# A hybrid encoder layer on one core: queries and keys stored as fp16 parts, and the order of its first stages

## The chip, the cores and the metric

The kernel runs on one core of a Trainium2 chip. The metric is the device time of one execution in microseconds (us). Three runs of the kernel before took 2835.52 to 2839.13 us, median 2836.63. A separate execution was recorded by the hardware profiler; all lines of the profile come from it. The engines are PE (TensorE: matmuls; PEld is its weight load), DVE (VectorE), ACT (ScalarE), POOL (GpSimd) and SP (SyncE, which issues most DMAs). Each engine works through its own instructions in order.

## The reference

One layer on x of 2048 tokens by 1024, with 256 memory tokens:

```python
y = rmsnorm(x, g_mix) @ w_in                     # q, k, v (512 each), a, g (512 each)
q, k = partial_rotary(q), partial_rotary(k)      # 8 heads of 64, the first 16 of each head turned
att = dilated_sliding_attention(q, k, v)         # windows (128,1), (512,4), (2048,16), softmax-weighted
u = a * sigmoid(g); conv = silu(layernorm(depthwise_conv31(u) + conv_b))
h = x + concat(att, conv) @ w_out
h = h + cross_attention(rmsnorm(h, g_x), rmsnorm(mem, g_mem)) @ w_xo     # 4 heads of 256
h = h + relu(rmsnorm(h, g_mlp) @ w_up)**2 @ w_down                       # 4096 hidden
out = rmsnorm(h, g_final)
```

The pattern (window, dilation) splits the tokens into `dilation` strided sequences; in each, a query sees keys at a distance of at most window / (2 x dilation) = 64.

## The kernel before

**Numbers.** Values that enter a matmul are split into two parts, high and low, and a product is three matmuls: high by high, high by low, low by high (`mm3`, L390 to L394). For the linear layers the parts are fp16, each tile scaled by a power of two. The scale is found on the chip: `pow2` (L194) takes a sum or maximum over a tile, its inverse root, and keeps the exponent. `wscale` (L325) does this for each 1024 x 128 tile of w_in by itself, with a DVE pass, a small matmul `p`, a POOL power and DVE steps. `wsplit2` (L377) writes the high part on ACT (L379) and the low part on DVE (L380); `wsplit_views` (L345) does it with a permutation of columns for the rotary tiles (L347 to L350). The queries and keys are the exception: they are kept as fp32r (fp32 bits, read by TensorE as fp32r) high and low parts, each key tile holding high rows in partitions 0 to 63 and low rows in 64 to 127, so a score takes two matmuls (L1112 and L1113 for the dilation 16, L1258 for the others), of 256 or 128 columns each.

**Stages, by the time of the profiled execution.**
- 0 to about 131 us: projections of the memory (`memory`, L554), in fp32r, with `xprep` (L528) of the first two quarters of x: load 512 tokens, norm, transpose, split into fp16 parts, and write the transposed x back (xscr).
- to about 230: the gated units `glu` 0 and 1 (L722; a unit g and a unit a, each 1024 x 128 weights times 512 tokens, for two quarters of x), with `xprep` of the other two quarters.
- to about 440: `lin_qk` (L845), eight units: kr and qr hold the first 16 dimensions of every head (rotary), k0, q0, k1, q1, k2, q2 the other 48. Each loads its weight tile, scales and splits it, multiplies it with four quarters of x, turns the rotary ones (L906 to L910), and splits the result (keys L927 and L928, queries L919 and L920). It stores the parts to DRAM: kscr (keys, ordered by token modulo 16), qscr (queries), qfar (queries ordered by token modulo 16). ACT issues the stores of the high parts, SP those of the low parts. The far tiles are stored in two halves. The rope tables are loaded for kr and again for qr.
- Beside these units run, woven in by rates: `scan` (L220), which loads all of w_up and w_out in 40 tiles of 512 KB and squares them on ACT (sjunk, L227) to bound the scales; `vscale` (L761), column norms of the v weights (two halves squared on ACT, added on POOL, summed by matmuls vss, L778); and the first quarter of the convolution (DVE, L409).
- to about 548: glu 2, v for the first two pairs of heads' halves (`lin_v`, L789), glu 3, the first half of the second v unit, whose weights are written to vscr and read back (wvr) for the second half.
- to about 780: the attention of the first 512 queries together with the dilation 16 for all queries (`att`, `att_far`, L1093), woven with the rest of v and of the gated units.
- from about 780: four `post` stages (L1488), each output projection, cross-attention and MLP for 512 tokens, woven with the attention and convolution of the next 512. In the first of them `scan_down` (L242) loads w_down in 32 tiles (scand) and squares them on ACT (L249).

**What sets the order.** The program is written as generators that `pipeline`, `weave` and `run` interleave by hand-set rates; `pinned` and `after` tie an instruction behind the last one of an engine. A scheduler then orders the instructions of each engine, with the tiles of the pools as constraints: a tile with 3 buffers can be loaded again only when its third-last use is over. SP issues its DMAs in that fixed order, so a load that waits for a buffer holds up all loads behind it; ACT, too, holds up a weight split behind a square that waits for its load.

All DMAs are issued by one helper, so most show as L58.

Of the kernel before, what the change touches and what calls it, by code (L numbers as in the profile page):

```python
# [10 lines left out]
F32 = mybir.dt.float32  # L11
# [37 lines left out]
def hybrid_layer(ctx, tc, A, out):  # L49
# [58 lines left out]
    kscr = dr.tile([2, HD, H, 16, 160], F32R, name="kscr")  # L108
    qscr = dr.tile([2, HD, H, S], F32R, name="qscr")
    qfar = dr.tile([2, HD, H, 16, P], F32R, name="qfar")  # L110
# [39 lines left out]
    cst.tile([P, 96], F32, name="cpad")  # L150
# [82 lines left out]
    def loads_ahead(gens):  # L233

        next(gens[0])
        for i, g in enumerate(gens):
            if i + 1 < len(gens):
                next(gens[i + 1])
            yield
            next(g, None)  # L240
# [238 lines left out]
    xna[2] = pool("x2", stack=mems, side="right")  # L479
    mwp = pool("memw", stack=mems, side="right")  # L480
# [15 lines left out]
    def load_nat(sp, src, name, bufs=10):  # L496

        t = [sp.tile([P, 512], F32, tag="nat", name=f"{name}_{e}", bufs=bufs) for e in range(2)]
        for e in range(2):
            dma(t[e], src[:, 512 * e:512 * e + 512])  # L500
        return t
# [26 lines left out]
    def xprep(sp, n):  # L528
        xtiles(n)
        nat = [load_nat(sp, A["x"][0, 512 * n + P * j:512 * n + P * (j + 1), :], f"xn{n}_{j}") for j in range(4)]  # L530
        r = rstd_nat(sp, nat, f"x{n}")
        rb = ps("c", f"rb{n}")
        bcast_rows(rb, r, 4)
        rbs = sp.tile([P, 512], F32, tag="rbs", name=f"rbs{n}", bufs=1)
        ACT.copy(rbs, rb)
        yield
        for k in range(KC):
            pt = ps("a", f"xt{n}_{k}")
            for j in range(4):
                PE.transpose(pt[:, j * P:(j + 1) * P], nat_cols(nat[j], k), ident)  # L540
            xt = sp.tile([P, 512], F32, tag="xt", name=f"xts{n}_{k}", bufs=3)
            DVE.tensor_copy(xt, pt)
            dma(xscr[k][:, 512 * n:512 * (n + 1)], xt)
            xv = sp.tile([P, 512], F32, tag="xv", name=f"xv{n}_{k}", bufs=2)
            DVE.scalar_tensor_tensor(xv, pt, gmix[:, k:k + 1], rbs, op0=ALU.mult, op1=ALU.mult)
            ACT.copy(XH_[k, n], xv)
            POOL.tensor_tensor(XL_[k, n], xv, XH_[k, n], op=ALU.subtract)
            yield

# [4 lines left out]
    def memory(sp):  # L554
# [24 lines left out]
        def wtiles(name, shape=(P, 8, P)):  # L579
            i = cnt[0] % 4  # L580
            cnt[0] += 1
            if i < 2:
                return [pl.tile(list(shape), dt, tag=t, name=f"m{t}_{name}", bufs=b)
                        for pl, t, dt, b in ((wp, "raw", F32, 3), (mwp, "whi", F32R, 2), (mwp, "wlo", F32R, 2))]
            return [xpool(q, j, 2, f"m{q}{j}_{name}", shape, dt)
                    for q, j, dt in (("h", i - 2, F32), ("h", i, F32R), ("l", i, F32R))]
# [174 lines left out]
    def vscale():  # L761

        for pr in range(4):
# [6 lines left out]
            POOL.tensor_tensor(sq[0], sq[0], sq[1], op=ALU.add)  # L770
            POOL.tensor_tensor(sq[0][:, 0:2], sq[0][:, 0:2], sq[0][:, 2:4], op=ALU.add)
            yield
            yield
            with ExitStack() as st:
                after(st, "pe", "dve")
                pc = ps("c", f"vss{pr}")
                for q in range(2):
                    PE.matmul(pc[:, 0:1], sq[0][:, q], ones[:, 0:1], start=q == 0, stop=q == 1)  # L778
# [65 lines left out]

    def lin_qk(isq, c):  # L845

        base = 0 if isq else DATT
        nm = f"{'q' if isq else 'k'}{c}"
        key = ("q" if isq else "k", c)
        v = w_in.rearrange("(k p) m -> p k m", p=P)  # L850
        raw = wp.tile([P, 8, P], F32, tag="raw", name=f"raw_{nm}", bufs=3)
        if c == "r":
            for k in range(KC):
                dma(raw[:, k, :].rearrange("p (h j) -> p h j", j=16),
                    v[:, k, base:base + DATT].rearrange("p (h d) -> p h d", d=HD)[:, :, 0:16])
            yield
            yield from wscale(raw, key)
            yield
            views = [(lambda t, x=x: t.rearrange("p k (h x j) -> p k h x j", x=2, j=8)[:, :, :, x, :],
                      lambda t, x=x: t[:, :, x * 64:(x + 1) * 64].rearrange("p k (j h) -> p k h j", h=H))  # L860
                     for x in range(2)]
            hi, lo = two(wsplit_views(raw, wcol(key, 0), nm, views))
        else:
            for p, h, d, m in segs(c):
                dma(raw[:, :, p:p + m], v[:, :, base + h * HD + d:base + h * HD + d + m])
            yield
            yield from wscale(raw, key)
            yield
            hi, lo = two(wsplit2(wp, raw, nm, wcol(key, 0)))

        def rope(n):
            t = []
            for i in range(2 if c == "r" else 0):
                t.append(t2(f"rope{i}_{nm}{n}"))
                dma(t[i], A["rope"][i, :, 512 * n:512 * (n + 1)])
            return t

        nxt = rope(0)
        yield

        def store(d, t, tail, q=None):

            if c != "r":
                for p, h, d0, m in segs(c):
                    dma(f(d[(slice(d0, d0 + m), h) + tail]), f(t[p:p + m]), q)
            else:
                v = d[(slice(0, 16), slice(0, H)) + tail]
                dma(f(v.rearrange("d h s -> (d h) s" if len(tail) == 1 else "d h r i -> (d h) r i")), f(t), q)

        w = 64 if isq else 80  # L890
        for n in range(NG):
            hf = n // 2
            i0 = 0 if isq or hf else PADI
            if n % 2 == 0:
                far = [lbk.tile([P, 16, 80], F32R, tag=f"st{x}", name=f"st{x}_{nm}{hf}", bufs=2)[:, :, 0:w] for x in "hl"]
                if not isq:
                    for t in far:
                        POOL.memset(f(t[:, :, 64:] if hf else t[:, :, 0:PADI]), 0.0)
            rc = nxt
            if n + 1 < NG:  # L900
                nxt = rope(n + 1)
            pt = linear(hi, lo, n)
            if c == "r":
                ct, sn = rc
                sw = t2(f"sw_{nm}{n}")
                ACT.copy(sw[0:64], pt[64:128])  # L906
                ACT.copy(sw[64:128], pt[0:64])
                last["dve"] = DVE.tensor_tensor(ct, pt, ct, op=ALU.mult)
                POOL.tensor_tensor(sn, sw, sn, op=ALU.mult)
                POOL.tensor_tensor(ct, ct, sn, op=ALU.add)  # L910
# [3 lines left out]
            sl = slice(i0 + 32 * (n % 2), i0 + 32 * (n % 2) + 32)  # L914
            fh, fl = (t[:, :, sl].rearrange("p r i -> p i r") for t in far)
            if isq:
                o = t2(f"qh_{nm}{n}", F32R)
                l = lbk.tile([P, 512], F32R, tag="ql", name=f"ql_{nm}{n}", bufs=3)
                ACT.activation(o, src, AF.Copy, scale=wcol(key, 2))  # L919
                last["dve"] = DVE.scalar_tensor_tensor(l, src, wcol(key, 2), f(o), op0=ALU.mult, op1=ALU.subtract)  # L920
                cols = (slice(512 * n, 512 * (n + 1)),)
                for z, (t, ft) in enumerate(((o, fh), (l, fl))):
                    store(qscr[z], t, cols, None if z else nc.scalar)
                    POOL.tensor_copy(f(ft), f(t).rearrange("p (i r) -> p i r", r=16))
# [945 lines left out]
```

## Time and profile before

| | us |
|---|---|
| median of 3 runs | 2836.63 |
| lowest, highest | 2835.52, 2839.13 |
| profiled execution | 2834.45 |
| its span, first to last instruction | 2832.7 |
| PE busy | 2692.5 |
| DVE busy | 2063.9 |
| ACT busy | 1311.4 |
| POOL busy | 451.7 |

The mean granted clock of TensorE over the span is 0.974; 462.09 MB are moved. The page gives busy time by engine, the span in 40 slices of 70.8 us, the DMA queues (q1 is SP's, q10 ACT's), and the chain of work that ended last. The windows view gives the busy time of each engine in a stretch that is asked for, with the granted clock and the share of the 16 DMA engines that was busy (it can come out a little over 1). The line view groups instructions by line, engine and operation: busy time, mean ns of one, and idle time ahead of them with what ended it. The view of waits sums such idle time by pair. A matmul's duration includes its way through the array; consecutive ones overlap, so PE's busy time is less than their sum.

### The profile page before, as it was taken

The page shows a single profiled execution, that of the slowest core. Times are in us where ns is not written, and L with a number is a line of the kernel's source. Part 1 is how long each engine was busy: PE and PEld are TensorE (multiplying, and loading weights), DVE is VectorE, ACT ScalarE, POOL GpSimd, SP SyncE. Part 2 cuts the span into 40 slices and gives each one's busy share as a digit, 9 for nine tenths or more (in the row PEclk, how much of TensorE's full clock was granted, in tenths as well). Part 3 has the DMA queues.
Part 4 walks back from the last instruction along what each step waited for, and adds up shares of the span by engine and source line. Part 5 has one row for each costly group of instructions (what it writes and reads, how often), then busy time and mean ns, then how long its engine had stood idle before and what let it go on. Part 6 is the DMA issues. An engine that isn't in the chain of part 4 may idle for free.

```text
span 2832.7 us, 41746 instructions
## 1 busy us (share of the span) xinstructions
PE 2692.5 (95%) x15482; PEld 1486.3 (52%) x15482; DVE 2063.9 (73%) x3757; ACT 1311.4 (46%) x2169; POOL 451.7 (16%) x499
## 2 busy tenths in 40 slices
PE   8877899899878999999999999999999999999998
PEld 7743346677644554544555555455455544444443
DVE  6765675655557998766898876579988656579997
ACT  5646321165557543453554345345443444455443
POOL 1024431121210211130011203100201130000000
PEclk9988899999998999999999999999999999999999
DMA  9899996559887544455444455454445355233341
GB/s 274 264 264 277 252 219 173 173 167 239 208 274 226 142 132 128 138 148 149 148 130 129 132 145 146 139 170 119 131 137 141 120 152 157 97 90 100 116 119 60
DMA packets 624045, 462.09 MB, mean 163 GB/s; under 512 B 192893, under 2 KB 550193, under 8 KB 623072
## 3 DMA queue, kind: packets, MB, share of 16 engines
q1 hardware_dynamic: 583088, 435.48, 53.8%
q10 hardware_dynamic: 38528, 17.93, 2.5%
q0 software_dynamic: 2224, 6.01, 0.6%
q8 instruction: 122, 2.00, 0.3%
q14 instruction: 83, 0.68, 0.1%
HBM read 371.09 MB, written 88.23 MB: 162 GB/s over the span
## 4 chain that ended last, share of the span: by engine, by line
PE 76%; DMA 9%; DVE 6%; ACT 3%; issue 2%; SPq 2%; POOL 1%; ACTq 1%; POOLq 0%; DVEq 0%
PE up L392 7%; PE up L393 7%; PE up L394 7%; PE dn L392 7%; PE dn L394 7%; PE dn L393 7%; PE pt L1036 2%; PE s L1258 2%; PE lin L392 2%; PE lin L393 2%; PE xs L392 2%; PE xs L393 2%; PE x L392 2%; PE xs L394 2%; PE x L393 2%
## 5 line engine op out<-in xcount | busy, mean ns | idle before, releaser
L392 PE MATMUL up<-mh,ws_u 128*128 128x512 f16 x1024 | 389.6, 381 | 2.6 <-DVE rl L1593 2.6
L393 PE MATMUL up<-ml,ws_u 128*128 128x512 f16 x1024 | 389.4, 380 | 0.0
L394 PE MATMUL up<-mh,ws_u 128*128 128x512 f16 x1024 | 388.3, 380 | 0.0
L409 DVE SCALAR_TENSOR_TENSOR cacc<-cu,cw,cacc 128x512 f32<-128x512 f32 x480 | 379.0, 790 | 4.6
L393 PE MATMUL dn<-hhl,ws_d 128*128 128x512 f16 x768 | 290.2, 379 | 0.3 <-DVE hhl L1596 0.3
L394 PE MATMUL dn<-hhh,ws_d 128*128 128x512 f16 x768 | 290.1, 379 | 0.0
L392 PE MATMUL dn<-hhh,ws_d 128*128 128x512 f16 x768 | 283.2, 379 | 0.8 <-DVE h L1609 0.8
L379 ACT ACTIVATE ws_u<-raw_u,bd 128x1024 f16<-128x1024 f32 x128 | 146.8, 1147 | 244.8 <-PE dn L394 199.7
L379 ACT ACTIVATE ws_d<-raw_d,bd 128x1024 f16<-128x1024 f32 x100 | 114.9, 1149 | 280.7 <-PE up L394 248.7
L1609 DVE SCALAR_TENSOR_TENSOR h<-dn,bd,h 128x512 f32<-128x512 f32 x192 | 140.7, 746 | 63.8 <-PE dn L394 62.9
L380 DVE SCALAR_TENSOR_TENSOR ws_u<-raw_u,bd,ws_u 128x1024 f16<-128x1024 f32 x128 | 168.4, 1315 | 18.2 <-ACT ws_u L379 17.7
L1029 DVE CUSTOM_DVE_ANT_0 sm<-s,mask 128x256 f32<-128x256 f32 (+1 forms) x384 | 128.2, 375 | 57.0 <-PE s L1258 38.3
L1593 DVE SCALAR_TENSOR_TENSOR rl<-up,ssumx 128x512 f32<-128x512 f32 x96 | 65.7, 689 | 135.1 <-PE up L394 135.0
L394 PEld LDWEIGHTS <-ws_u 128*128 128x128 f16 x1024 | 100.5, 98 | 120.4 <-issue 1.6
L393 PEld LDWEIGHTS <-ws_u 128*128 128x128 f16 x1024 | 100.9, 99 | 116.7 <-issue 4.0
L392 PEld LDWEIGHTS <-ws_u 128*128 128x128 f16 x1024 | 100.6, 98 | 115.6 <-issue 1.6
L1030 ACT ACTIVATE sm<-sm,o 128x256 f32<-128x256 f32 (+1 forms) x288 | 114.8, 452 | 99.5 <-DVE o L1029 98.9
L380 DVE SCALAR_TENSOR_TENSOR ws_d<-raw_d,bd,ws_d 128x1024 f16<-128x1024 f32 x100 | 134.5, 1345 | 29.1 <-ACT ws_d L379 28.4
L367 POOL TENSOR_TENSOR nr<-st_v,mhalf 128x4 f32<-128x4 f32 (+1 forms) x15 | 14.8, 987 | 807.0 <-DVE st_v L363 807.0
L1040 DVE TENSOR_TENSOR pl<-pt,ph 128x512 f16<-128x512 f32 x160 | 109.4, 685 | 46.1 <-ACT ph L1039 45.9
L394 PEld LDWEIGHTS <-ws_d 128*128 128x128 f16 x768 | 75.1, 98 | 89.1 <-issue 0.6
L1039 ACT CAST ph<-pt 128x512 f16<-128x512 f32 x160 | 91.3, 572 | 61.0 <-PE pt L1036 60.6
(549 smaller groups left out, 6724.7 us busy)
## 6 DMA issues: line engine op xcount, KB each, us to landing
raw_u<-in_w_up_dram SPq DMA_DIRECT2D x128, 512.0 KB
raw_d<-in_w_down_dram SPq DMA_DIRECT2D x100, 512.0 KB
scan<-in_w_up_dram SPq DMA_DIRECT2D x32, 512.0 KB
raw_o<-in_w_out_dram SPq DMA_DIRECT2D x32, 512.0 KB
scand<-in_w_down_dram SPq DMA_DIRECT2D x32, 512.0 KB
raw_a<-ascr SPq DMA_DIRECT2D x32, 512.0 KB
raw_b<-bscr SPq DMA_DIRECT2D x32, 512.0 KB
b<-in_w_down_dram SPq DMA_DIRECT2D x28, 512.0 KB
```

What stands on the lines that cost most here:

```text
L379: ACT.activation(t[:, 0], raw, AF.Copy, scale=scale)
L380: DVE.scalar_tensor_tensor(t[:, 1], raw, scale, t[:, 0], op0=ALU.mult, op1=ALU.subtract)
L392: PE.matmul(o, lh, rh, start=first, stop=False, skip_group_check=more)
L393: PE.matmul(o, lh, rl, start=False, stop=False, skip_group_check=more)
L394: last["pe"] = PE.matmul(o, ll, rh, start=False, stop=end, skip_group_check=more)
L409: DVE.scalar_tensor_tensor(acc, u[:, t:t + 512], cw[:, c, t:t + 1], acc, op0=ALU.mult, op1=ALU.add)
L1029: last["dve"] = DVE.tensor_tensor_reduce(dst, so, mask[:, 256 * m:256 * m + nk], 1.0, 3e38, ALU.add, ALU.min, mn)
L1030: last["act"] = ACT.activation(dst, dst, AF.Exp, bias=mn, scale=-1.0)
L1039: ACT.copy(ph, pt)
L1040: DVE.tensor_tensor(pl, pt, ph, op=ALU.subtract)
L1593: last["dve"] = DVE.scalar_tensor_tensor(r, pt, 0.0, rsb, op0=ALU.max, op1=ALU.mult)
L1609: last["dve"] = DVE.scalar_tensor_tensor(hs[m], pt, K_DN, hs[m], op0=ALU.mult, op1=ALU.add)
```

## The change

Five things are changed.

1. **fp16 parts.** kscr, qscr and qfar and all tiles of queries and keys become fp16, high and low. So that one scale serves all tiles of the queries and one all tiles of the keys, the eight weight tiles are loaded first (`qk_load`), each one's maximum of squares goes to a column of `qkn`, and one matmul and two `pow2` give the scales for all (`qks`). The results are scaled so that the scores come out with a common factor, which the mask step multiplies away (`SCORE`, in place of 1.0).
2. **Stores.** Each far tile covers all 2048 tokens and is stored once, in place of two halves. The rope tables are loaded once and used by kr and qr.
3. **Order.** glu 0, 1 and 2 come first, then the eight units of queries and keys, then glu 3 and v. `wqk` holds the eight raw weight tiles from early on (before that, the parts of the memory weights lie there).
4. **x.** `xprep` takes both quarters of a pair and loads the second while the first is worked on; the natural-layout tiles have 16 buffers in place of 10, and the third quarter's tiles of the memory weights no longer lie in x's pools.
5. **Squares and sums.** `scan` is woven in at 0.4 in place of 0.75 per step during the query and key units, faster after them; the first quarter's convolution is one sequence. In `vscale` the two POOL adds are gone and eight small matmuls per pair sum the squares.

```diff
-    kscr = dr.tile([2, HD, H, 16, 160], F32R, name="kscr")
-    qscr = dr.tile([2, HD, H, S], F32R, name="qscr")
-    qfar = dr.tile([2, HD, H, 16, P], F32R, name="qfar")
+    kscr = dr.tile([2, HD, H, 16, 160], F16, name="kscr")
+    qscr = dr.tile([2, HD, H, S], F16, name="qscr")
+    qfar = dr.tile([2, HD, H, 16, P], F16, name="qfar")
...
+    wqk = pool("wqk", stack=early, side="right")
+    mrw = pool("memraw", stack=mems, side="right")
...
-    def xprep(sp, n):
-        xtiles(n)
-        nat = [load_nat(...) for j in range(4)]
-        r = rstd_nat(sp, nat, f"x{n}")
+    def xprep(sp, ns):
+        nat = xload(sp, ns[0])
+        yield
+        for n in ns:
+            xtiles(n)
+            r = rstd_nat(sp, nat, f"x{n}")
+            yield
+            nxt = xload(sp, n + 1) if n + 1 in ns else None
...
-            POOL.tensor_tensor(sq[0], sq[0], sq[1], op=ALU.add)
-            POOL.tensor_tensor(sq[0][:, 0:2], sq[0][:, 0:2], sq[0][:, 2:4], op=ALU.add)
...
-                for q in range(2):
-                    PE.matmul(pc[:, 0:1], sq[0][:, q], ones[:, 0:1], start=q == 0, stop=q == 1)
+                for q in range(8):
+                    PE.matmul(pc[:, 0:1], sq[q // 4][:, q % 4], ones[:, 0:1], start=q == 0, stop=q == 7)
...
+    def qk_load():
+        v = w_in.rearrange("(k p) m -> p k m", p=P)
+        def one(i, c, isq):
+            base = 0 if isq else DATT
+            raw = wqk.tile([P, 8, P], F32, tag=f"q{i}", name=f"qkw{i}")
+            qkraw[isq, c] = raw
+            if c == "r":
+                for k in range(KC):
+                    dma(raw[:, k, :]..., v[:, k, base:base + DATT]...[:, :, 0:16])
+            else:
+                for p, h, d, m in segs(c):
+                    dma(raw[:, :, p:p + m], v[:, :, base + h * HD + d:base + h * HD + d + m])
+            yield
+            j = (i // 2) + (0 if isq else 4)
+            DVE.tensor_tensor_reduce(q, w, w, 1.0, 0.0, ALU.mult, ALU.max, qkn[:, j:j + 1])
+        gens = [one(i, c, isq) for i, (c, isq) in enumerate(...)]
+        yield from loads_ahead(gens, 3)
+        ...
+            PE.matmul(pc[:, 0:8], onesq, qkn, start=True, stop=True)
+        pow2(v[:, 4:6], v[:, 6:8], None, 32768.0, "dve", of=v[:, 0:2])
+        pow2(v[:, 8:10], v[:, 10:12], None, 181.0, "dve", of=v[:, 2:4])
...
-            yield from wscale(raw, key)
...
+            for n in range(0 if isq else NG):
+                for i in range(2):
+                    ropes[n, i] = lbk.tile([P, 512], F32, tag=f"rope{n}{i}", name=f"rope{n}{i}")
+                    dma(ropes[n, i], A["rope"][i, :, 512 * n:512 * (n + 1)])
...
-            if n % 2:
-                for z, t in enumerate(far):
-                    store((qfar if isq else kscr)[z], t, (slice(0, 16), slice(w * hf, w * hf + w)),
-                          None if z else nc.scalar)
+            if n == NG - 1:
+                for y, t in enumerate(far):
+                    store((qfar if isq else kscr)[y], t, (slice(0, 16), slice(0, w)), None if y else nc.scalar)
...
-        run([mg, chain(xprep(sp, 0), xprep(sp, 1))], (3, 1))
+        run([mg, xprep(sp, (0, 1))], (3, 1))
...
-        units = list(chain(glu(0, early01), glu(1, early01)))
+        units = [u for c in range(3) for u in glu(c, early01)]
         units += [lin_qk(isq, c) for c in ("r", 0, 1, 2) for isq in (False, True)]
-        steps = pipeline(*units, *glu(2, early01), lin_v(0, alln), *glu(3, early01), lin_v(1, early01))
+        steps = pipeline(*units, *glu(3, early01), lin_v(0, alln), lin_v(1, early01))
+        qkl = qk_load()
...
-        weave(islice(steps, 7), (later, 2.5))
-        drain(later)
+        weave(islice(steps, 9), (later, 2), (qkl, 1.2))
+        drain(later, qkl)
...
-        weave(islice(steps, 31), (vsc, 0.42), (conv0, 0.58), (scn, 0.75))
+            weave(islice(steps, 2), (vsc, 0.4))
+            weave(islice(steps, 32), (vsc, 0.4), (conv0, 0.78), (scn, 0.4))
...
-        weave(islice(steps, 4), (scn, 1))
-        weave(islice(steps, 8), (conv0, 1.1), (scn, 1))
-        weave(islice(steps, 4), (conv0, 0.25), (scn, 1))
-        weave(steps, (conv0, 2), (scn, 2))
+        weave(islice(steps, 3), (scn, 2))
+        weave(steps, (conv0, 1.05), (scn, 2.2))
...
-        last["dve"] = DVE.tensor_tensor_reduce(dst, so, mask[...], 1.0, 3e38, ALU.add, ALU.min, mn)
+        last["dve"] = DVE.tensor_tensor_reduce(dst, so, mask[...], SCORE, 3e38, ALU.add, ALU.min, mn)
...
-        k = p2_.tile([P, 16, 144], F32R, tag="k3", name=f"k3_{h}", bufs=2)
-        dma(f(k), f(kscr[:, :, h].rearrange("x d r i -> (x d) r i")[:, :, 0:144]))
+        k = p2_.tile([P, 16, 160], F16, tag="k3", name=f"k3_{h}", bufs=2)
+        dma(k, kscr[:, :, h].rearrange("x d r i -> (x d) r i"))
```

`scan_down`, the `post` stages, `att_far` and `att` keep their code but for the types.

202 lines of the change are left out of this document (100 added, 102 removed).

## The prediction

> **What bounds the kernel now.** I read the page first, for the engine that is nearly full, then the windows, for the stages in which it is not.
>
> ```profile
> PE 2692.5 (95%) x15482; PEld 1486.3 (52%) x15482; DVE 2063.9 (73%) x3757; ACT 1311.4 (46%) x2169; POOL 451.7 (16%) x499
> PEclk9988899999998999999999999999999999999999
> DMA  9899996559887544455444455454445355233341
> PE 76%; DMA 9%; DVE 6%; ACT 3%; issue 2%; SPq 2%; POOL 1%; ACTq 1%; POOLq 0%; DVEq 0%
> ```
>
> TensorE is the bound over the run; the DMA engines are full in the first fifth only. So a saved transfer is worth something early, and matmul time is worth something everywhere. The windows say how much can be had in each stage. Their columns: the stretch, its length, busy us of PE, PEld, DVE, ACT, POOL, then the granted clock, the DMA share and GB/s.
>
> ```profile
> 120.00:320.00 200.00, 147.69 (x646) 76.01 (x645) 124.62 (x241) 105.77 (x163) 76.23 (x68) 0.83 1.02 274
> 320.00:450.00 130.00, 127.58 (x599) 58.97 (x598) 82.11 (x140) 33.75 (x43) 51.75 (x59) 0.99 0.92 219
> 540.00:640.00 100.00, 89.01 (x761) 70.45 (x762) 58.19 (x215) 48.27 (x114) 16.82 (x24) 0.91 0.59 165
> 640.00:780.00 140.00, 129.70 (x1177) 100.11 (x1174) 79.07 (x327) 77.31 (x195) 28.17 (x50) 0.95 0.87 222
> 780.00:900.00 120.00, 93.41 (x528) 49.59 (x529) 77.51 (x153) 76.34 (x139) 14.24 (x15) 0.89 0.87 274
> 900.00:1300.00 400.00, 397.21 (x2261) 205.69 (x2259) 316.27 (x525) 183.03 (x282) 78.64 (x77) 1.00 0.49 139
> ```
>
> I take as loss of a stage its length less busy time times clock, since an idle TensorE comes back at a lower clock. That gives 200 - 147.69 x 0.83 = **77 us** in 120 to 320 (gated units, first key and query units), 4 in 320 to 450, 19 and 17 in the attention stage from 540, **37** in 780 to 900 (the first post stage) and 3 in the 400 us after that. The change can win idle time in three places, and nothing but matmul time after 900.
>
> The chain of waits (start, us, what) says what the front waits for:
>
> ```profile
> 168.94 4.89 DMA scan<-in_w_up_dram
> ...
> 206.33 7.10 DMA xn<-in_x_dram
> ...
> 225.77 4.71 ACT ws_kr L349 x2
> 230.52 0.61 PE lin L392
> ...
> 280.86 6.28 DMA rope_qr<-in_rope_dram
> ...
> 314.35 2.42 ACTq L58
> 316.81 1.15 ACT sjunk L227 x2
> 317.96 1.05 ACT ws_q L379
> ```
>
> ScalarE runs in order: a square of w_up (L227) whose tile has not landed holds up the weight split behind it, and so the matmuls; the x tiles of 206 stand behind those tiles on SP. At 314 to 317 it is the issue of key stores on ScalarE's own queue that holds the split of q0.
>
> **The change part by part.**
>
> *Gated units first, tiles loaded ahead, squares later.* In the issue order of the changed program, ScalarE's part, 15 squares instead of 21 stand ahead of the first key split (L349), and glu 2 with its 96 matmuls stands ahead of it too. By the first row below, where 20 us at full clock hold 96 matmuls, that is 20 us of TensorE work pulled out of the part after 440 into the starved part.
>
> ```profile
> 240.00:260.00 20.00, 20.00 (x96) 9.24 (x94) 8.20 (x9) 11.52 (x20) 10.78 (x11) 1.00 0.96 231
> 300.00:320.00 20.00, 5.98 (x27) 2.75 (x26) 10.78 (x22) 8.12 (x12) 5.52 (x8) 0.72 1.08 285
> ```
>
> The price is paid in transfers, for the stage is full (share 1.02, 274 GB/s). Added ahead of the first key unit on SP's queue: five more 512 KB projection tiles (before, kr, qr and k0 stood there) and the two of glu 2, 7 x 0.52 = 3.7 MB. Taken away: six squares, 3.1 MB, and the loads of the third 512 tokens of x, 2.1 MB, which move up into the memory stage. Net -1.5 MB, about -5 us at 274 GB/s. SP is in order, and all eight tiles stand ahead of the last tile of glu 1, so I count that gain as lost to the wait for that tile. The first key unit then still starts near 230, with 20 us more done: **-20**.
>
> *Stores halved, rope loaded once.* The DMA view for 280 to 440 (packets, MB, share) and the issue rows of the run:
>
> ```profile
> q1 hardware_dynamic: 52626, 24.52, 60.8%
> q10 hardware_dynamic: 32642, 12.52, 34.0%
> ```
>
> ```profile
> rope_qr<-in_rope_dram SPq DMA_DIRECT2D x8, 256.0 KB
> k<-kscr SPq DMA_DIRECT2D x24, 512.0 KB
> ```
>
> ScalarE's queue moves 12.5 MB in 34% of 160 us, 230 GB/s. With SP's equal half the key and query stores come to some 25 MB; half of them at that rate is 54 us of DMA time, the second rope load (8 x 0.26 = 2 MB) 9 more: 63 us. Key and far stores also go from two issues per tile to one. In 320 to 450 TensorE loses 4 us already, so there these 63 us buy almost nothing. They pay in 240 to 320, where the sum of length less busy times clock is 24 us (the row of 300 to 320 alone loses 16). With the rope wait and the store convoy ahead of L379 gone, what is late next is the squares still on ScalarE and the split itself; I keep 10 us: **-14**. Ends for the whole front: -60 (three quarters of 77 + 4) and 0 (glu 2 waits for its weights behind the tiles loaded ahead).
>
> The granted clock deserves a second reading. The Trainium skill, "TensorE: Matmul & The Clock Gate", Part 1, says that the clock is either half or full, and that a warm-up lasts some 3.4 us. With nine idle stretches in 120 to 320 that makes at most 9 x 1.7 = 15 us lost beside the 52 us of idleness, an estimate from that page; the row gives 147.69 x 0.17 = 25. By the page the front would give some 4 us less than I count. The measured row decides.
>
> *Scores from fp16 parts.* 768 matmuls lose fp32r operands. From the line view of L1258 (min/median/max ns) and the groups by form:
>
> ```profile
> L1258 PE MATMUL s<-k,ql x256: 277/286/477, 585.1 to 2241.7; 128*128 128x256 f32 x128
> ```
>
> ```profile
> L1258 PE MATMUL s<-k,qh 128*128 128x256 f32 x160 | 58.5, 380 | 1.7 <-DVE low L1029 1.6
> L394 PE MATMUL v<-wv,xl 128*128 128x256 f16 x192 | 52.0, 273 | 0.0
> L1112 PE MATMUL s<-k,qh 128*128 128x256 f32 x128 | 40.1, 343 | 2.5 <-DMA qh<-qfar 2.5
> L1258 PEld LDWEIGHTS s<-k,ql 128*128 128x128 f32 x256 | 53.6, 209 | 2.8
> L393 PEld LDWEIGHTS <-hqh 128*128 128x128 f16 x112 | 11.0, 98 | 13.1 <-issue 0.4
> ```
>
> By the median, 768 x (286 - 273) = 10 us; by the mean of the slowest group, 380, the means would allow 30 and more, but much of that is clock and waiting. The weight load shrinks from 209 to 98 ns, beside other matmuls either way. The loaded query columns are picked out with a stride of 4 in the first attention stage, the streamed keys in runs of 8 values, which no fp16 row here shows: if that load took the fp32 row's 209 ns and its extra 111 ns showed for one matmul in four, 21 us would be added. Ends -30 and +11; I take **-10**, by the median, the nearest row.
>
> *The norm sums of v.* POOL's adds go, and 8 tiny matmuls become 32:
>
> ```profile
> L778 PE MATMUL vss<-ones,vsq 128*128 128x1 f32 x12 | 1.5, 229 | 0.0
> ```
>
> 24 x 1.5/12 = **+3**, in a stage where TensorE is full. Eight tiny scale matmuls (p) fewer take 1 us back; not counted. The scale in the mask step (L1029) is a per-partition column in place of 1.0: no row separates these; I cost it at 0, since DVE, busy 316 of 400 us after 900, has 84 us there to hide it in.
>
> *What moves without being named.* In the issue order of the changed program all 32 loads of scand (squares of w_down, L249) stand during the second half of v and the first third of the far attention; before, the chain meets them in the first post stage.
>
> ```profile
> L249 ACT ACTIVATE sjunkd<-scand 128x1024 bf16<-128x1024 f32 x32 | 33.8, 1055 | 21.7 <-DMA scand<-in_w_down_dram 21.6
> ```
>
> ```profile
> 818.79 4.07 DMA scand<-in_w_down_dram
> ...
> 838.10 6.29 DMA scand<-in_w_down_dram
> ```
>
> The first post stage loses 37 us; it sheds 16.8 MB (61 us at its 274 GB/s), 34 us of ScalarE work and the 21.6 us that ScalarE waited. I keep 17 of the 37 for the waits that no scand appears in: **-20** (ends -35 and 0). In exchange 540 to 640 receives them: ScalarE has 48.27 of 100 busy there and would have 82, and the DMA share of 0.59 would be near 1.2 with nothing halved. I put **+8** on that (ends 0 and +60, below). The wait before the reloaded v weights is among the 19 us lost there; its load keeps its place in SP's order, so it stays:
>
> ```profile
> PE v L392 <- DMA wvr<-vscr: 10.9, 1, 10.9
> ```
>
> Halved key reads (24 x 512 KB, 6 MB less) fall where TensorE loses little: **-2**, out of the 17 us of 640 to 780.
>
> Sum: -20 - 14 - 10 + 3 - 20 + 8 - 2 = **-55**. The profiled execution took 2834.45 (span 2832.7), 2.2 under the median of the runs, 2836.63. So 2779.5 on its scale, and **2781** or 2782 against the median; I take 2781.
>
> **The rivals.**
>
> *The front stays bound by DMA* (chance 0.18): eight tiles ahead of glu 1's last tile starve glu 1 and 2, and the key units start 20 us later. For it: share 1.02, SP in order. Against: fewer bytes stand ahead. Then the -34 shrinks to -10: 2805.
>
> *Both places open wider* (0.13): the front gives 50 and the first post stage 35: 2781 - 16 - 15 = 2750; with scores at -20, 2740.
>
> *Slower: the w_down squares block the far attention* (0.14). SP takes a scand load only when a buffer of the two is free, which needs a square on ScalarE; ScalarE waits in order for that load, ahead of exponentials (L1030) and casts (L1039) that TensorE needs. Key loads stand behind on SP. Seven such pieces, of 4.1 to 6.3 us, lie on the chain in the first post stage. All 32, each a square of 1055 ns and half of a 5.8 us load, would be 126 us of ScalarE's queue; 540 to 640 leaves ScalarE 52 us free, and some of the rest lies beside TensorE work that is already fed: +60, and +80 with the clock lost after each idle stretch. With +80 in place of +8 and the other terms as forecast the time is 2853. It decides from the point where the block costs more than the 63 us that the other terms give.
>
> *The change doesn't do what it says* (inside the 0.18): fp16 scores run no faster and the squares stay ahead. 15 instead of 21 speaks only half for it.
>
> **How the numbers follow.** Forecast 0.55 (2755 to 2797), DMA-bound front 0.18, wider 0.13, slower 0.14. The range 2735 to 2822 takes in the wide front and post ends, and the front at 0 with the other terms kept (2815); it leaves out the slower rival and the tails. A measurement of this kernel tells about 0.2%, 5.7 us, from no change; faster takes the first three cases less 0.03 and slower the last less 0.01, which fall within that band: 0.83, same 0.04, slower 0.13.
>
> **What would show it.** Front: in the changed profile the first split of kr ends near 230 with glu 2 already done, and length less busy times clock over 120 to 320 is 40 or below; 60 or more refutes the step. Stores: half of the 12.5 MB on ScalarE's queue over the key and query units. Scores: the L1258 groups near 273 ns median. w_down: sjunkd leaves 780 to 900, whose loss falls to about 17, and the loss of 540 to 640 stays below 30. Wrong most of all if that last figure is above 60, or if TensorE's idle time before the gated weights grows with the tiles loaded ahead.

## The result, and the profile after

The changed kernel takes 2823.95 us (median of 7 runs, 2818.97 to 2825.87), the kernel before 2836.0 us (7 runs beside them): a ratio of 0.9957, 95% interval 0.9945 to 0.997. It is faster by 12 us, where 55 were forecast, and lies 2 us above the stated range. In what follows a difference between two kernels is the difference of their ratios to the kernel before, times 2836.

The page of the changed kernel, the same lines as shown of before:

```profile
PE 2682.1 (95%) x15516; PEld 1455.5 (52%) x15516; DVE 2123.5 (75%) x3723; ACT 1330.1 (47%) x2169; POOL 462.0 (16%) x485
PEclk9989998899999999999999999999999999999999
DMA  9999544577753444454444445454445355233341
```

The DMA engines are no longer full after the fourth slice: the halved stores show. But VectorE is busy for 60 us longer than before, though it has fewer instructions (3723 against 3757). The windows view says where (columns as before):

```profile
120.00:320.00 200.00, 167.28 (x771) 84.83 (x771) 142.25 (x244) 122.51 (x183) 89.62 (x66) 0.91 0.93 260
320.00:450.00 130.00, 114.19 (x518) 54.13 (x517) 122.59 (x125) 36.46 (x27) 62.72 (x36) 0.91 0.39 99
540.00:640.00 100.00, 73.65 (x572) 53.31 (x572) 38.33 (x165) 50.41 (x113) 5.68 (x15) 0.90 0.80 223
780.00:900.00 120.00, 105.25 (x676) 57.48 (x674) 86.53 (x187) 56.26 (x105) 16.60 (x25) 0.96 0.49 141
```

Length less busy time times clock: 48 us in 120 to 320 (77 before), 26 in 320 to 450 (4), 34 in 540 to 640 (19), 19 in 780 to 900 (37). The front won most of what it should (29 of 34 us) and two other stages gave it back. In 320 to 450 VectorE is busy 122.6 of 130 us, against 82 before: a new bound, in a stage whose DMA share fell from 0.92 to 0.39. In 540 to 640 TensorE, VectorE and POOL are all idle more than before.

Windows cut at fixed times mix stages that have shifted, so I also use four points of the program: the last matmul of the query units (ws_q), of the reloaded v weights (wvr), the first of the output projection (ws_o) and of w_up (ws_u). The tile view gives first and last start at the end of a row. The kernel before, then the changed one:

```profile
L392 PE MATMUL lin<-xh,ws_q x96: 376/379/634, 319.0 to 426.1; 128*128 128x512 f16 x96
L392 PE MATMUL v<-wvr,xh x64: 272/273/421, 547.8 to 570.1; 128*128 128x256 f16 x64
L392 PE MATMUL o<-cath,ws_o x256: 376/379/634, 781.2 to 2415.6; 128*128 128x512 f16 x128
L392 PE MATMUL up<-mh,ws_u x1024: 376/379/634, 966.0 to 2802.4; 128*128 128x512 f16 x171
```

```profile
L395 PE MATMUL lin<-xh,ws_q x96: 376/379/634, 310.3 to 446.4; 128*128 128x512 f16 x96
L395 PE MATMUL v<-wvr,xh x64: 272/273/421, 554.0 to 589.6; 128*128 128x256 f16 x64
L395 PE MATMUL o<-cath,ws_o x256: 376/379/631, 795.1 to 2402.2; 128*128 128x512 f16 x128
L395 PE MATMUL up<-mh,ws_u x1024: 376/379/634, 958.7 to 2789.0; 128*128 128x512 f16 x171
```

| us spent | before | forecast | after | writes and squares mended (e6) |
|---|---|---|---|---|
| to the last ws_q | 426.1 | 415 | 446.4 | 418.7 |
| to the last wvr | 144.0 | 124 | 143.2 | 123.9 |
| to the first ws_o | 211.1 | 212 | 205.5 | 187.5 |
| to the first ws_u | 184.8 | 165 | 163.6 | 178.0 |
| to the end of the span | 1866.7 | 1862 | 1860.3 | 1859.7 |

The forecast column is the sum's terms put in their places (glu 2's 20 us are in the first row of every column but that of before). The first two rows missed by 50 us; the fourth and fifth are right; the third is better than forecast, as the point-by-point account explains.

**What fills VectorE.** The line view of VectorE from 320 to 450, the changed kernel:

```profile
L412 DVE SCALAR_TENSOR_TENSOR cacc<-cu,cw,cacc 128x512 f32<-128x512 f32 x69 | 77.8, 1127 | 1.6
L959 DVE SCALAR_TENSOR_TENSOR stl_k<-lin,qks,sth_k 128x512 f16<-128x512 f32 x11 | 26.9, 2480 | 1.4 <-ACT sth_k L958 1.4
```

and before:

```profile
L409 DVE SCALAR_TENSOR_TENSOR cacc<-cu,cw,cacc 128x512 f32<-128x512 f32 x48 | 43.3, 903 | 0.5
L928 DVE SCALAR_TENSOR_TENSOR stl_k<-lin,wsc,sth_k 128x512 fp32r<-128x512 f32 x10 | 10.6, 1079 | 0.0
```

Two things are seen. The write of a key's low part takes 2480 ns in place of 1079, with the same number of elements and half the bytes: the tile is written token by token, and neighbouring tokens lie 320 bytes apart, so each 2-byte value goes to a place of its own. (The instruction also reads the high part, sth_k, which lies the same way.) And there are 69 conv steps in place of 48, of a mean 1127 ns in place of 903. The chain of waits (start, us, what) shows single steps, and the timeline of POOL what ran beside them (in brackets, POOL's idle time ahead of it):

```profile
343.45 0.67 DVE cacc L412
...
344.15 2.20 DVE cacc L412
...
346.37 0.76 DVE cacc L412
```

```profile
343.58 2.84 POOL L955 COPY stl_q<-ql_q 128x512 f16<-128x512 f16 x1 [4.11 <-issue]
```

The conv step that starts after POOL's copy of the queries (343.58 to 346.42) ends with it, at 346.35, and takes three times as long as its neighbours. The Trainium skill, "SBUF — State Buffer", section "SBUF: two separate sides", says that a VectorE instruction with two inputs in SBUF and a GpSimd instruction that reads SBUF need the same pair of ports, which the one that starts first holds to its end. A conv step and a copy are such a pair, and the trace agrees that the step waits: of the 84 conv steps between 290 and 470 us, the 26 that start during one of these copies all end within 0.1 us of the copy's recorded end and take 2.15 us in the mean, the other 58 take 0.78. This copy, too, writes scattered 2-byte values: 2.84 us.

**What stalls the attention.** The chain from 554 on:

```profile
554.33 13.66 DMA scand<-in_w_down_dram
...
568.07 1.15 ACT sjunkd L252 x2
...
569.25 5.70 DMA scand<-in_w_down_dram
...
575.03 1.15 ACT sjunkd L252 x2
```

It goes on like that to 608: load of a w_down tile, square on ScalarE, next load. ScalarE's other work waits behind the squares, and TensorE for ScalarE. The wait view of the squares:

```profile
ACT sjunkd L252 <- DMA scand<-in_w_down_dram: 34.6, 22, 7.5
```

34.6 us in 540 to 680, where the first post stage of the kernel before had 19.2 us of such waits.

### The profile page after: what moved, and what is told of

Read it like the earlier page. It is cut to its first block, busy times and chain, and to the rows that moved or that the text cites. A ratio compares the mean times of both kernels' runs of the same rounds, so it can differ in the third digit from the quotient of the medians.

```text
span 2819.0 us, 41539 instructions
## 1 busy us (share of the span) xinstructions
PE 2682.1 (95%) x15516; PEld 1455.5 (52%) x15516; DVE 2123.5 (75%) x3723; ACT 1330.1 (47%) x2169; POOL 462.0 (16%) x485
## 4 chain that ended last, share of the span: by engine, by line
PE 69%; DVE 14%; DMA 6%; issue 3%; ACT 3%; SPq 1%; POOL 1%; DVEq 0%; POOLq 0%; ACTq 0%
PE dn L395 7%; PE dn L396 7%; PE dn L397 7%; PE up L395 7%; PE up L396 7%; PE up L397 7%; DVE cacc L412 4%; DMA scand<-in_w_down_dram 2%; PE xs L395 2%; PE xs L396 2%; PE xs L397 2%; PE pt L1065 2%; PE o L395 2%; PE o L397 2%; PE o L396 2%
## 5 line engine op out<-in xcount | busy, mean ns | idle before, releaser
L412 DVE SCALAR_TENSOR_TENSOR cacc<-cu,cw,cacc 128x512 f32<-128x512 f32 x480 | 405.0, 844 | 5.2
L1058 DVE CUSTOM_DVE_ANT_0 sm<-s,mask,qks 128x256 f32<-128x256 f32 (+1 forms) x384 | 150.4, 434 | 45.5 <-PE s L1287 33.9
L1065 PE MATMUL pt<-ident,sm 128*128 128x128 f32 x640 | 102.9, 277 | 20.7 <-ACT sm L1059 17.0
```

Of the source, the lines that this page charges most:

```text
L412: DVE.scalar_tensor_tensor(acc, u[:, t:t + 512], cw[:, c, t:t + 1], acc, op0=ALU.mult, op1=ALU.add)
L1058: last["dve"] = DVE.tensor_tensor_reduce(dst, so, mask[:, 256 * m:256 * m + nk], SCORE, 3e38, ALU.add, ALU.min, mn)
L1065: last["pe"] = PE.transpose(pt[:, j, :], sm[:, j, :], ident)
```

## The experiments

Theory after the result: (1) the scattered 2-byte writes make VectorE the bound from 320 to 450, and (2) the early squares of w_down cost the attention about what they save the post stage. Rivals: the convolution's new place alone fills VectorE; the early squares are a gain. The times are medians of 4 to 8 executions.

| run | edit on | us | ratio, 95% interval |
|---|---|---|---|
| after | | 2823.95 | 0.9957, 0.9945 to 0.997 |
| e1_along | after | 2791.82 | 0.9848, 0.9832 to 0.9863 |
| e2_conv | after | 2793.64 | 0.9855, 0.9838 to 0.9872 |
| e3_scand | after | 2805.33 | 0.9895, 0.9881 to 0.9909 |
| e4_dtype | before | 2828.05 | 0.9972, 0.996 to 0.9984 |
| e7_dtype_scand | e4 | 2806.59 | 0.9912, 0.9897 to 0.9927 |
| e6_along_scand | e1 + e3 | 2768.86 | 0.9776, 0.9762 to 0.9789 |
| e5_all | e6 + e2 | 2777.68 | 0.9803, 0.9789 to 0.9818 |
| e9_glu2 | e6 | 2800.98 | 0.9888, 0.9874 to 0.9902 |
| e10_room | e1 | 2778.06 | 0.9805, 0.9787 to 0.9823 |
| e11_vss | e6 | 2765.89 | 0.976, 0.9742 to 0.9779 |
| e12_keys | e6 | 2781.32 | 0.9814, 0.9797 to 0.9832 |
| e13_queries | e6 | 2781.04 | 0.9811, 0.9794 to 0.9829 |

**e1_along: the same values written in runs.**

```diff
-            fh, fl = (t[:, :, i0 + 32 * n:i0 + 32 * n + 32].rearrange("p r i -> p i r") for t in far)
+            fh, fl = (t[:, :, i0 + 32 * n:i0 + 32 * n + 32] for t in far)
...
-                    POOL.tensor_copy(ft, t.rearrange("p (i r) -> p i r", r=16))
+                    POOL.tensor_copy(ft, t.rearrange("p (i r) -> p r i", r=16))
...
-                s3 = src.rearrange("p (i r) -> p i r", r=16)
+                s3 = src.rearrange("p (i r) -> p r i", r=16)
```

> Only the order in which the far tiles are written changes: each fp16 part is written in runs of 32 neighbouring values instead of one value every 320 bytes. Theory (the scattered 2-byte writes make VectorE the bound from 320 to 450 us: stl_k 2.46 us against 1.08 before, and conv steps of 2.2 us beside the POOL copies): stl_k near 1.1 us, conv steps 0.75 us throughout, the loss of 320 to 450 (length less busy times clock) falls from 26 us to below 12, the run is 12 to 22 us faster than the changed kernel, near 2806. Rival (the whole first quarter of the convolution now lies in that stage, and that alone fills VectorE): the durations may fall but the stage stays within 5 us, near 2820. Second rival (any 2-byte access at a stride is slow, reads too): stl_k stays above 2 us and nothing moves.

31 us faster than the changed kernel, more than the 12 to 22 expected. VectorE's lines from 320 to 450 and the window:

```profile
L412 DVE SCALAR_TENSOR_TENSOR cacc<-cu,cw,cacc 128x512 f32<-128x512 f32 x66 | 58.5, 887 | 1.5
...
L959 DVE SCALAR_TENSOR_TENSOR stl_k<-lin,qks,sth_k 128x512 f16<-128x512 f32 x10 | 7.5, 747 | 6.9 <-ACT sth_k L958 6.9
```

```profile
320.00:450.00 130.00, 130.00 (x662) 65.34 (x660) 93.57 (x133) 22.57 (x30) 41.89 (x47) 1.00 0.50 133
```

747 ns for the same write, and TensorE is full at full clock. The source is read in permuted order now, and that costs nothing: ql_q, of the same shape but not permuted, takes 748 ns here, and on ScalarE both have a median of 687. (On VectorE the edit also puts the reading of the high part in runs, so there the write alone was not separated from it; ScalarE's write has no such second input.) The conv steps still have a mean of 887 ns: POOL's copies take less time, but the 22 steps that start during one still take 1.37 us.

**e2_conv: the convolution back at its old rates.**

```diff
-            weave(islice(steps, 32), (vsc, 0.4), (conv0, 0.78), (scn, 0.4))
+            weave(islice(steps, 32), (vsc, 0.4), (conv0, 0.45), (scn, 0.4))
...
-        weave(steps, (conv0, 1.05), (scn, 2.2))
+        weave(steps, (conv0, 1.9), (scn, 2.2))
```

> Only the weaving rates of the first quarter's convolution change: 0.78 to 0.45 beside the query and key units, 1.05 to 1.9 after them, about as the kernel before had it. Rival (placement of the convolution fills VectorE): 15 to 20 us faster than the changed kernel, near 2806, the loss of 320 to 450 below 10. Theory (slow writes fill it): 5 to 10 us faster, near 2816, since some 26 conv steps of 0.75 us leave, but stl_k stays at 2.46 us.

29 us, beyond the rival's 15 to 20 as well, with stl_k still at 2.47 us. So in the new order either cure lifts the bound: with the conv steps moved, VectorE is busy for 102 of the 130 us and TensorE for 128. The two theories were not exclusive; e5 tells them apart.

**e3_scand: the squares held.** The instructions that square w_down are tied behind the last exponential that the program has issued.

```diff
-            dsc = scan_down(pp)
+            dsc = pinned(scan_down(pp), "act")
```

> The squares of w_down are held behind ScalarE's exponentials of the first post stage, so all but the first two loads go back there. Theory (the early loads cost the attention stage about what they save the first post stage): the loss of 540 to 680 falls by some 20 us, that of the first post stage rises by some 18, the run within 6 us of the changed kernel, 2818 to 2828. Rival (the early loads are a net gain, as the prediction had it, -20 and +8): 10 us or more slower, 2834 or more.

18 us faster, so the early squares were a net loss, and more of one than the theory said. The window and the points:

```profile
540.00:640.00 100.00, 87.29 (x775) 66.37 (x773) 51.81 (x216) 45.48 (x106) 17.98 (x26) 0.93 0.51 148
```

```profile
L395 PE MATMUL v<-wvr,xh x64: 272/273/417, 556.3 to 578.3; 128*128 128x256 f16 x64
L395 PE MATMUL o<-cath,ws_o x256: 376/379/634, 767.2 to 2388.1; 128*128 128x512 f16 x128
L395 PE MATMUL up<-mh,ws_u x1024: 376/379/634, 946.1 to 2774.8; 128*128 128x512 f16 x171
```

The first ws_o comes 28 us earlier than in the changed kernel (767.2 against 795.1), the first ws_u only 13 us earlier (946.1 against 958.7): the early squares cost 28 us up to the post stage and save 15 in it. By the profiled executions the net is 14 us, 1.5 of it after the first ws_u; by the ratios of all runs it is 18.

**e4_dtype and e7_dtype_scand: the types alone.** The kernel before with F16 in place of F32R in every query and key tile, stores, scales and orders as before; then with the squares held.

```diff
-    kscr = dr.tile([2, HD, H, 16, 160], F32R, name="kscr")
+    kscr = dr.tile([2, HD, H, 16, 160], F16, name="kscr")
...
-                far = [lbk.tile([P, 16, 80], F32R, tag=f"st{x}", name=f"st{x}_{nm}{hf}", bufs=2)[:, :, 0:w] for x in "hl"]
+                far = [lbk.tile([P, 16, 80], F16, tag=f"st{x}", name=f"st{x}_{nm}{hf}", bufs=2)[:, :, 0:w] for x in "hl"]
```

> The kernel before with nothing but fp16 in place of fp32r for the query and key parts (scales per tile, two half stores and all orders as before). Theory: the stage of 320 to 450 has 48 us of VectorE time free before, the slow writes take most of it, so it loses little; scores save 6 to 10 us in the attention stages: 5 to 15 us faster than before, near 2826, with stl_k near 2.4 us. Rival (the fp16 parts and their smaller stores were worth 20 us or more, and the reordering lost them): 2815 or less. Other rival (the parts themselves are the loss, since the writes are slow): 2836 or more.

> The kernel before with fp16 parts alone, and the w_down squares held. Theory (smaller query and key tiles free room in the on-chip memory for the post stage's tiles, so the squares move up in any order of the rest; the cost is the same): 10 to 20 us below the fp16 parts alone (2828), 2808 to 2818. Rival (the early squares hurt only beside the new order): within 4 us of 2828.

8 us faster than before, and 25 with the squares held. The total of e4 is as expected, but not its parts: the stage of 320 to 450 was to lose little, and it loses 19 us (4 before).

```profile
320.00:450.00 130.00, 119.43 (x537) 54.43 (x536) 101.50 (x133) 36.93 (x33) 73.19 (x53) 0.93 0.63 132
```

The last ws_q starts at 441.7, 16 us later than before, though the convolution has its old rates and VectorE is busy for only 101.5 of the 130 us. So the scattered writes cost time in the old order without filling VectorE; the chain there passes from POOL's copies to the key writes on ScalarE and VectorE and to conv steps, and which of them costs it was not separated. In e4 stl_k takes 2.4 us, and sjunkd begins at 575 in place of 801, in an order that is otherwise the old one: it is the smaller tiles that bring the squares forward. In e7 the far attention (last wvr to first ws_o) takes 185 us against 211 before:

```profile
L392 PE MATMUL v<-wvr,xh x64: 272/273/421, 563.1 to 585.7; 128*128 128x256 f16 x64
L392 PE MATMUL o<-cath,ws_o x256: 376/379/634, 770.9 to 2393.9; 128*128 128x512 f16 x128
```

**e6_along_scand and e5_all: the cures together.** e6 has the edits of e1 and e3, e5 those of e2 too.

> Writes in runs of 32 values and the w_down squares held, together. Theory (the slow writes cost 32 us and the early squares 19, in different stages): the two add up, 2824 - 32 - 19 = 2773 (2768 to 2778), the loss of 120 to 900 near 95 us. Rival (both are one wait, moved along: with the writes fixed the attention stage starts earlier and finds other cover): 2782 or more.

> The same and the convolution's first quarter at the old rates. Theory (slow writes and placement fill the same VectorE, so either cure is enough): within 4 us of the kernel with writes and squares alone, 2769 to 2777. Rival (each has its own share): 10 us or more below it, 2763 or less.

e6 is 51 us faster than the changed kernel, about the sum of 31 and 18: the two faults lie in different stages, and neither hides the other. e5 was expected within 4 us of e6 and is 8 slower. With the writes cured, the change's own place for the convolution is the better one: e2's gain was room for VectorE, not a better order.

**e12_keys and e13_queries: whose writes.** Both are e6 with one half of e1's edit undone: in e12 POOL's copies of the queries scatter again, in e13 the keys' writes on ScalarE and VectorE.

```diff
-                    POOL.tensor_copy(ft, t.rearrange("p (i r) -> p r i", r=16))
+                    POOL.tensor_copy(ft.rearrange("p r i -> p i r"), t.rearrange("p (i r) -> p i r", r=16))
```

```diff
+                fh, fl = (t.rearrange("p r i -> p i r") for t in (fh, fl))
                 ACT.activation(fh, s3, AF.Copy, scale=ev)
```

(e13 reads s3 in token order again.)

> The kernel with writes and held squares, but only the keys written in runs; POOL's copies of the queries scattered again. Theory (VectorE time is what counts: some 18 conv steps lose 1.45 us each beside such copies, 26 us, of which the free VectorE time of the stage hides a part): 5 to 15 us above 2769, conv steps near 2.2 us again beside the copies. Rival (only the keys' own writes on ScalarE and VectorE matter): within 3 us of 2769.

> The other half: only the queries' copies in runs, the keys scattered again (stl_k 2.46, sth_k 2.75 us). Theory: 12 x 1.7 us more on VectorE and 12 x 2 us on ScalarE, partly hidden: 3 to 12 us above 2769. Rival (only the blocked conv steps matter): within 3 us of 2769.

11 and 10 us above e6; both scattered cost 34 (e3 against e6). The conv steps' row from 320 to 450, e12 and then e13:

```profile
L412 DVE SCALAR_TENSOR_TENSOR cacc<-cu,cw,cacc 128x512 f32<-128x512 f32 x71 | 79.7, 1123 | 1.6
```

```profile
L412 DVE SCALAR_TENSOR_TENSOR cacc<-cu,cw,cacc 128x512 f32<-128x512 f32 x72 | 67.2, 933 | 1.6
```

VectorE is busy for 93.6 of the 130 us in e6, 112.5 in e12 and 114.4 in e13: both halves load it, and the second one costs more than the first, as when slack has been used up. e13 slows ScalarE's writes too; how its 10 us divide between the two engines was not separated.

**e9_glu2: glu 2 back behind the query and key units,** with the convolution's channels 2 and 3, which need it.

```diff
-        units = [u for c in range(3) for u in glu(c, early01)]
+        units = [u for c in range(2) for u in glu(c, early01)]
...
-        steps = pipeline(*units, *glu(3, early01), lin_v(0, alln), lin_v(1, early01))
+        steps = pipeline(*units, *glu(2, early01), *glu(3, early01), lin_v(0, alln), lin_v(1, early01))
```

> The kernel with contiguous writes and held squares, but glu 2 and the convolution's channels 2 and 3 back behind the query and key units, as before. Theory (glu 2's 20 us of TensorE work fill idle time in the starved front): 12 to 22 us slower than that kernel, near 2790, with the first kr matmul at most 8 us earlier. Rival (the front ends when its transfers end, whatever TensorE does): within 4 us of it.

32 us slower than e6, more than the 12 to 22 expected; 8 of them can be the convolution's place (e5), so some 24 are glu 2's. The front does hide its 20 us: the last ws_q starts at 415.6 without glu 2 ahead of it and at 418.7 with it (e6). In 120 to 320 TensorE does less in the same time:

```profile
120.00:320.00 200.00, 158.80 (x706) 80.72 (x706) 138.00 (x245) 116.48 (x187) 84.88 (x70) 0.85 0.98 262
```

**e10_room: 8 KB of unused space.** No order is pinned; the far attention's pool is made larger by about what fp16 had freed there.

```diff
-        p2_.tile([P, 176], F32, name="farpad")
+        p2_.tile([P, 176 + 2048], F32, name="farpad")
```

> Writes in runs of 32 values, and 8 KB per partition of unused space added to the far attention's pool, about what the halved key and query tiles had freed there; no order is pinned. Theory (the early squares come from that freed room: without it, the w_down tiles share space with the attention's tiles and must wait for them): sjunkd goes back to the first post stage by itself and the run equals the one with writes and held squares, 2764 to 2774. Rival (the early squares have another cause, or the gain of holding them comes from the pinned order): sjunkd still begins near 536, or the time stays near 2792.

The squares' row in the changed kernel, then here:

```profile
L252 ACT ACTIVATE sjunkd<-scand x32: 1040/1056/1062, 566.7 to 668.7; 128x1024 bf16<-128x1024 f32 x32
```

```profile
L252 ACT ACTIVATE sjunkd<-scand x32: 1039/1057/1067, 751.7 to 851.0; 128x1024 bf16<-128x1024 f32 x32
```

They go back to the post stage by themselves: the freed room was what let the squares in early. The time falls by 12 us against e1, not by the 20 that the pinned order brings (2778 against 2769, outside the expected 2764 to 2774). What makes the other 8 was not separated.

**e11_vss: POOL's adds back.**

```diff
+            POOL.tensor_tensor(sq[0], sq[0], sq[1], op=ALU.add)
+            POOL.tensor_tensor(sq[0][:, 0:2], sq[0][:, 0:2], sq[0][:, 2:4], op=ALU.add)
...
-                for q in range(8):
-                    PE.matmul(pc[:, 0:1], sq[q // 4][:, q % 4], ones[:, 0:1], start=q == 0, stop=q == 7)
+                for q in range(2):
+                    PE.matmul(pc[:, 0:1], sq[0][:, q], ones[:, 0:1], start=q == 0, stop=q == 1)
```

> The kernel with writes and held squares (2769), but the POOL adds of the v norms back and 8 tiny matmuls in place of 32. By the prediction's step (24 x 127 ns on a full TensorE): 3 us faster, 2764 to 2768. Rival (the adds hold VectorE's shared access and POOL's stores): no change or slower, 2769 to 2774.

4.5 us faster (3 by the medians, as the step said), but the intervals overlap: not told apart from no change. It is the fastest of all, 0.976 of the kernel before.

## Why the prediction was wrong, point by point

- **Front, order (-20): right.** The first kr matmul starts at 236 (forecast: near 230) with glu 2 done, the loss of 120 to 320 fell from 77 to 48 us, and e9 gives some 24 us for glu 2's place. The mark of 40 or below was not reached.
- **Front, stores (-14): in keeping with e6 and e9, gone in the changed kernel.** ScalarE's queue moves 5.93 MB from 280 to 440 in place of 12.52, and the DMA share of 320 to 450 fell to 0.39. The last ws_q stands at 418.7 in e6, against 415 by the sum, and at 415.6 in e9, 10 us ahead of the kernel before with glu 2 behind it in both (the tiles loaded ahead and the later squares have a part in that). The stores and the rope tables were not tested by themselves. In the changed kernel the last ws_q stands at 446.4.
- **What was never priced: writing the parts.** The prediction costed the fp16 parts at their matmuls, stores and loads, and the writes that make them (stl_k, sth_k, POOL's copies) at nothing, with no name for the cover. They went from 1.08 to 2.46 us and the like. This is the first failed step: 31 us (e1 against after), 28 of them seen in the table's first row (446.4 against 418.7 in e6). The second half of the cover was in a quoted row, VectorE's 82 of 130 us; the change itself put 21 more conv steps there, and its rate of 0.78 was read as order and not as load.
- **w_down squares in the attention (+8): the second failed step.** The mechanism stood in the text as the slower rival, priced at +80 and given 0.14; its size was 28 us up to the first ws_o (e3), some 13 of them ahead of the last wvr, in the table's second row. The loss of 540 to 640 came out at 34 us, above the 30 that it set as a bound.
- **First post stage (-20): right in size.** First ws_o to first ws_u went from 184.8 to 163.6; with the squares back (e3) 178.9, so 15 of the 21 are theirs. Together the move was forecast at -12 and measured at +18.
- **Scores (-10): too small.** The medians of L1287 are 272 ns (286 before), as counted.

```profile
L1287 PE MATMUL s<-k,ql x256: 269/272/415, 611.0 to 2228.3; 128*128 128x256 f16 x128
```

But these durations overlap; what TensorE gives up is the time from one start to the next. A run of scores whose query columns are picked out with a stride of 4, from the matmul ahead of it to the one behind it, in the kernel before and in the changed one (start, us, what):

```profile
640.10 0.38 PE L394 MATMUL lin<-xh,wr_g 128*128 128x512 f16 x1
...
640.68 0.40 PE L1258 MATMUL s<-k,qh 128*128 128x256 f32 x1
640.92 0.40 PE L1258 MATMUL s<-k,ql 128*128 128x256 f32 x1
641.16 0.39 PE L392 MATMUL lin<-xh,wr_g 128*128 128x512 f16 x1
```

```profile
675.45 0.38 PE L397 MATMUL lin<-xh,wr_g 128*128 128x512 f16 x1
...
675.88 0.27 PE L1287 MATMUL s<-k,qh 128*128 128x256 f16 x1
675.99 0.27 PE L1287 MATMUL s<-k,ql 128*128 128x256 f16 x1
676.10 0.38 PE L395 MATMUL lin<-xh,wr_g 128*128 128x512 f16 x1
```

The run takes 1.06 us before and 0.65 after. Its weight loads take 0.33 us each before and 0.11 after, and the scores start 0.24 and 0.11 us apart: the prediction had these loads beside other matmuls either way, and before the change they were not hidden. Summed like this over all such runs, with or without a stride and with TensorE's idle time left out, the scores of the far attention (last wvr to first ws_o) take 13 us less than before, where 5 were forecast, and the later ones 6 less. That the time from the first ws_u to the end fell by 6 us, as forecast, is only partly theirs: 4 of those 6 lie there.
- **Halved reads (-2): not told apart.** With the squares held, the far attention takes 185 to 189 us in place of 211 (e7, e3, e6). 13 of these 22 to 26 us are the scores'; TensorE's idle time inside their runs falls by 4 more; the other 5 to 9, in a stretch whose granted clock rises from 0.95 to 0.99 and more, were not separated. In the changed kernel the squares took 17 back (205.5). That the third row of the table still came out near its forecast of 212 is luck: the scores' gain and the squares' cost were both put too low there.
- **v norms (+3): as forecast, not separated from nothing** (e11).

Added up: without the two faults the change earns 64 us (e6), 9 more than forecast, and the table has the surplus in the far attention (187.5 us where 212 were forecast); the scattered writes and the early squares together took 51 of it back, which leaves the 12 measured.

## What to carry to other kernels

When a type is made smaller, price the instructions that write it as well as those that read it: three engines wrote a permuted fp16 tile one value at a time, at more than twice the time of fp32, and on VectorE and ScalarE reading in permuted order while writing in runs cost nothing. Smaller tiles can also move what was held back by shared room; look in the new issue order for loads that have moved, and ask of each what waits behind it in order. When one engine's stage fills, two causes can each look like the whole cost: undo both, singly and together.

## What the hardware showed that was not expected

- A write of 512 values per partition, each to a place 320 bytes from the last: on VectorE 1080 ns as 4-byte values, 2461 as 2-byte ones, 746 as 2-byte values in runs of 32 (medians of stl_k before, after and in e1); on ScalarE 1119, 2753 and 687 (sth_k); on POOL, whose source has the same type, 1339, 2844 and 1570 (stl_q). On VectorE the second input lies like the output.
- A conv step on VectorE that starts during one of POOL's scattered fp16 copies lasts to the copy's end: 2.2 us in place of 0.75.
- A weight load of 128 columns picked with a stride of 4 took 0.33 us as fp32r and 0.11 as fp16; without a stride, 0.19 and 0.10.
